# Placing the attention steps of a hybrid decoder block one by one

## The chip, the cores and the metric

The kernel runs on one core of a Trainium2 chip. That core has five instruction streams: PE (TensorE, matmuls and transpositions; its weight loads are listed apart as PEld), DVE (VectorE), ACT (ScalarE), POOL (GpSimd) and SP (SyncE, which issues DMAs). The metric is the device time of one execution in microseconds (us), as the median of several runs. One execution was also taken by the hardware profiler; its page and its trace are what the prediction reads.

## The reference, cut to what matters

One layer of a decoder on 1024 tokens of width 1024. The normalised input is multiplied by one wide matrix, which gives the queries and keys of a sparse attention (NSA), the inputs of a retention layer, and two merge gates. Both mixers' outputs are gated, summed and projected, then an MLP follows. The change is in the attention, which computes this for each block of 128 queries and each of two groups `g` of four heads:

```python
sc = jnp.einsum('qghd,cgd->gqhc', qi, k_cmp).astype(jnp.float32) * scale      # compressed keys
p_c = jax.nn.softmax(jnp.where(valid[None, :, None, :], sc, NEG), axis=-1)
o_c = jnp.einsum('gqhc,cgd->qghd', p_c.astype(dt), v_cmp)
...
ss = jnp.einsum('qghd,gqkd->gqhk', qi, k_sel).astype(jnp.float32) * scale     # selected blocks
p_s = jax.nn.softmax(jnp.where(smask, ss, NEG), axis=-1)
o_s = jnp.einsum('gqhk,gqkd->qghd', p_s.astype(dt), v_sel)
...
sw = jnp.einsum('qghd,kgd->gqhk', qi, k_win).astype(jnp.float32) * scale      # window of 512
p_w = jax.nn.softmax(jnp.where(wmask[None, :, None, :], sw, NEG), axis=-1)
o_w = jnp.einsum('gqhk,kgd->qghd', p_w.astype(dt), v_win)
o = gi[..., 0:1] * o_c + gi[..., 1:2] * o_s + gi[..., 2:3] * o_w
...
mix = sigmoid(gate_a) * (nsa_out @ w_proj_a) + sigmoid(gate_b) * (ret_out @ w_proj_b)
```

There are 16 blocks of 64 keys and 16 are selected, so the selected branch sees all keys up to the query's own.

## The kernel before, in words

Before the attention stage the kernel has normalised the input (`bh`, `bl`: high and low part, since one float32 product is made of three products of rounded parts), computed retention, queries, keys and values, and stored the queries to memory. After it come the last gate tiles, the two projections, the output projection, and the MLP.

The attention stage works on 16 *units*: `units` runs over the query blocks `qb` from 7 down to 0, and for each over the two groups `g`, so unit `n` has `qb = 7 - n // 2`. A unit has these steps.

*Query split* (`prep_q`, L1105 on ACT, L1106 on DVE): the query tile is split into `QQ` and `ql`. There are two buffers of each.

*Scores* (`scores`, generator). For each of four heads the selected branch (`base` 1, keys `KKs`) is made of one or two *score groups*, and then the window branch (`base` 2, keys `KKw`) likewise; a group is two matmuls into one PSUM tile `S` of at most 512 columns (`psS`, four buffers). The compressed keys of a block lie in `KKw` behind the window's, so the last window group covers them too; `put_cmp` copies them there (ACT) for each `qb`. For each part of a group DVE adds the mask and takes the minimum of the negated scores (`smallest`, L1161). For a head with two groups a small DVE instruction combines both minima (L1196). Then ACT takes the exponentials with that bias and sums them up (`exponential`, L1165), out of PSUM into the tiles `pSa`, `pSb`, `pW` and `pC`. After two heads of a branch come the *scalings* (`weigh_sel`, `weigh_win`): DVE makes a factor for each row from sums and gates (`factors`, L1211 to L1213), and POOL multiplies the probabilities by it (`weigh`, L1216). In the last two units (`qb` 0) one group holds all three branches of a head.

*Value blocks* (`pv`, generator). For each block of 128 keys, first of the selected branch and then of the window branch with the compressed block ahead of the last: four transpositions of the heads' probabilities into one PSUM tile `pt` (`psT`, two buffers, L1303), a split into `ph` (ACT, L1304) and `pl` (DVE, L1305), and `PV_LAG` = 2 blocks later the two matmuls with the values into `O`. At the end ACT and DVE copy `O` out into `AT` (L1316, L1320).

*Gate tiles* (`gate_pieces`): 32 tiles of 512 columns in eight pieces of three matmuls each, independent of the attention, fill PE between these steps. 244 of the 256 pieces lie in this stage. A tile accumulates in one PSUM buffer `gps`; from tile 17 on (`GALT`) every odd one takes a buffer of `S`. ACT drains it (L1067). At the sixth piece of a tile `gate_w` splits the next weight, once for two tiles: 1024 columns on ACT (L191) and on DVE (L194).

What sets the order. PE executes in the order in which the program was written. For the other engines a scheduler of the compiler puts instructions in order by when they can start, with program order deciding between those that are ready; instructions in `tc.keep_in_program_order` stay behind everything written for their engine before. These are the gate splits on ACT from the third weight on, the combined minima (L1196), and, where the selected branch has two groups, the first window minimum.

The program order itself comes from a list. `place(it, n, lo, hi)` sets `n` evenly spaced times between `lo` and `hi` (in units), at each of which the generator `it` is advanced by one step; the list `todo` is sorted by time and worked off. `S_AT` gives for each kind of unit, relative to the unit's number, begin and end of the selected groups and a time for their last scaling, and the same for the window's. The first scaling of a branch, the combined minimum and the exponentials are part of the generator's group steps. `GATES` says how many gate pieces lie in each unit, evenly spaced; `GATE0` how many come first; `Q_AT` and `C_AT` are the times of the query split and the key copy; `V_END` and `V_LAST` the end of the value blocks.

```python
for n, (qb, g) in enumerate(units):
    ...
    it = scores(n, qb, g, u)
    for k, (lo, hi, w) in zip(n_scores(qb), S_AT[min(n, 1 + (7 - qb))]):
        place(it, k - 1, n + lo, n + hi)
        place(it, 1, n + w, n + w)
    it = pv(qb, g, u)
    place(it, n_pv(qb) - 1, n, n + 1 + V_END)
    ...
for ev in sorted(todo, key=lambda v: v[:2]):
    ...
```

## Time and profile before

| | us |
|---|---|
| median of 3 runs (lowest, highest) | 1544.66 (1544.12, 1545.6) |
| time of the profiled execution | 1543.7 |
| its span, first to last instruction | 1541.5 |
| PE with a matmul, of the span | 1523.3 |
| DVE, ACT, POOL busy, of the span | 1038.4, 710.7, 515.1 |
| attention stage, on the span | 356.7 to 733.7 |
| PE, DVE, ACT, POOL busy in it | 368.7, 278.7, 258.2, 129.9 |

The time of an execution is a little longer than its span, by 2.2 us here. A matmul is listed with its latency, which overlaps the next one's; so PE's busy time says how much of the stretch had some matmul under way, and not how fast matmuls followed one another. Distances between starts say that. PEld is the weight load ahead of each matmul; a matmul that waits is often seen as a weight load that waits. In a list of waits the engine and line that waited stand left of the arrow, and what ended the wait right of it.

### The profile page before, as it was taken

How to read it: one execution, taken by the hardware profiler on the slowest of the kernel's cores; microseconds unless marked ns; L12 is line 12 of the kernel's file. 1: busy time of each engine (PE TensorE's matmuls, PEld its weight loads, DVE VectorE, ACT ScalarE, POOL GpSimd, SP SyncE). 2: the span in 40 equal slices, each digit the busy share in tenths (PEclk: the TensorE clock that was granted, in tenths of full speed). 3: DMA queues.
4: the chain of work that ended last, by engine and by line, in shares of the span. 5: the costliest groups of instructions: out<-in, count | busy, mean ns of one | idle time of the engine just before them, and what ended most of it. 6: DMA issues, size and time to landing. Idle time of an engine off the chain costs nothing.

```text
span 1541.5 us, 21817 instructions
## 1 busy us (share of the span) xinstructions
PE 1523.3 (99%) x7529; PEld 1269.1 (82%) x7529; DVE 1038.4 (67%) x2000; ACT 710.7 (46%) x1574; POOL 515.1 (33%) x567
## 2 busy tenths in 40 slices
PE   9999999999999999999999999999999999999998
PEld 6888888898888787788888888888888888888887
DVE  6865661666778777775754378876666768786573
ACT  6653462555677667775421263222222244443452
POOL 4110011002233333333000014767777518723640
PEclk9999999999999999999999999999999999999999
DMA  5202215752111111111644433444444797573472
GB/s 207 90 18 65 59 45 131 210 173 69 55 42 36 62 42 42 63 62 63 232 137 157 138 127 104 151 150 150 151 151 151 245 342 262 199 250 123 143 276 93
DMA packets 101904, 202.85 MB, mean 132 GB/s; under 512 B 10714, under 2 KB 27490, under 8 KB 101730
## 3 DMA queue, kind: packets, MB, share of 16 engines
q1 hardware_dynamic: 100946, 199.30, 39.0%
q0 software_dynamic: 704, 1.90, 0.3%
q8 instruction: 59, 0.97, 0.2%
q14 instruction: 51, 0.42, 0.1%
q10 hardware_dynamic: 144, 0.26, 0.0%
HBM read 147.75 MB, written 53.61 MB: 131 GB/s over the span
## 4 chain that ended last, share of the span: by engine, by line
PE 87%; DVE 5%; ACT 3%; issue 3%; POOL 2%; DMA 0%; SPq 0%; POOLq 0%; ACTq 0%; DVEq 0%
PE mm L164 24%; PE mmu L164 21%; PE mmd L164 20%; PE gps L164 9%; PE O L164 3%; PE S L164 3%; PE pt L1303 3%; DVE pl L1305 1%; ACT pW L1165 1%; PE pc L164 1%; PE pO L164 1%; DVE S L1161 1%; ACT ph L1304 1%; PE tp L397 0%; PE pS L164 0%
## 5 line engine op out<-in xcount | busy, mean ns | idle before, releaser
L1460 DVE TENSOR_TENSOR wl<-raw,wh 128x1024 fp32r<-128x1024 f32 x134 | 218.7, 1656 | 88.7 <-ACT wh L1459 88.5
L1459 ACT ACTIVATE wh<-raw 128x1024 fp32r<-128x1024 f32 x134 | 136.6, 1054 | 156.0 <-PE mmd L164 100.1
L164 PE MATMUL mmd<-wl,wh 128*128 128x512 f32 (+1 forms) x464 | 177.2, 382 | 0.0
L164 PE MATMUL mmd<-wh 128*128 128x512 f32 (+1 forms) x464 | 177.2, 382 | 0.0
L164 PE MATMUL mmd<-wh,wl 128*128 128x512 f32 (+1 forms) x464 | 177.1, 382 | 0.0
L200 POOL TENSOR_SCALAR msq<-ssq 128x1 f32<-128x1 f32 (+1 forms) x32 | 7.7, 241 | 387.9 <-ACT h L206 223.3
L1161 DVE CUSTOM_DVE_ANT_0 S<-S,edge_m 128x512 f32<-128x512 f32 (+9 forms) x200 | 101.7, 516 | 32.9 <-PE S L164 27.7
L164 PE MATMUL mm<-wh,bh 128*128 128x512 f32 (+1 forms) x320 | 122.4, 382 | 0.1
L164 PE MATMUL mm<-wl,bh 128*128 128x512 f32 (+1 forms) x320 | 118.9, 372 | 0.4 <-DVE wl L499 0.4
L164 PE MATMUL mm<-wh,bl 128*128 128x512 f32 (+1 forms) x320 | 118.0, 373 | 0.0
L1305 DVE TENSOR_TENSOR pl<-pt,ph 128x512 fp32r<-128x512 f32 (+1 forms) x148 | 97.4, 660 | 25.3 <-ACT ph L1304 23.1
L164 PE MATMUL gps<-bh,wh 128*128 128x512 f32 x256 | 107.9, 421 | 0.0
L1304 ACT ACTIVATE ph<-pt 128x512 fp32r<-128x512 f32 (+1 forms) x148 | 85.2, 578 | 39.5 <-PE pt L1303 38.3
L164 PEld LDWEIGHTS mmd<-wh 128*128 128x128 f32 x464 | 87.2, 188 | 17.1
L164 PEld LDWEIGHTS mmd<-wh,wl 128*128 128x128 f32 x464 | 87.2, 188 | 17.0
L164 PEld LDWEIGHTS mmd<-wl,wh 128*128 128x128 f32 x464 | 87.2, 188 | 16.7
L164 PE MATMUL mmu<-bh,wh 128*128 128x512 f32 (+1 forms) x264 | 101.0, 383 | 0.0
L164 PE MATMUL mmu<-bl,wh 128*128 128x512 f32 (+1 forms) x264 | 100.9, 383 | 0.0
L164 PE MATMUL mmu<-bh,wl 128*128 128x512 f32 (+1 forms) x264 | 100.6, 383 | 0.0
L164 PE MATMUL gps<-bh,wl 128*128 128x512 f32 x256 | 100.6, 393 | 0.0
L164 PE MATMUL gps<-bl,wh 128*128 128x512 f32 x256 | 100.5, 393 | 0.0
L1216 POOL TENSOR_SCALAR pSa<-pSa,cf 128x512 f32<-128x512 f32 (+2 forms) x52 | 32.9, 646 | 133.7 <-DVE cf L1213 99.0
(381 smaller groups left out, 3999.2 us busy)
## 6 DMA issues: line engine op xcount, KB each, us to landing
raw<-u_scr SPq DMA_DIRECT2D x56, 512.0 KB, 4.4
raw<-w_down SPq DMA_DIRECT2D x41, 512.0 KB, 5.2
raw<-w_up SPq DMA_DIRECT2D x32, 512.0 KB, 3.9
u_scr<-u SPq DMA_DIRECT2D x60, 256.0 KB, 4.1
u_scr<-s SPq DMA_DIRECT2D x45, 256.0 KB, 2.3
y<-w_down SPq DMA_DIRECT2D x16, 512.0 KB, 7.0
x<-x SPq DMA_DIRECT2D x8, 512.0 KB, 4.8
raw<-w_ga SPq DMA_DIRECT2D x8, 512.0 KB, 3.9
```

What stands on the lines that cost most here:

```text
L164: T.matmul(o, w, m, start=start, stop=stop)
L200: G.tensor_scalar(m[:, :w], ssq, 1.0 / n, EPS, op0=OP.mult, op1=OP.add)
L1161: return V.tensor_tensor_reduce(sc, sc, mk, -0.125, BIGPOS, OP.add, OP.min, mx[:, i, b:b + 1])
L1165: A.activation(o, sc, AF.Exp, bias=mx[:, i, m:m + 1], scale=-1.0, accum_out=sums[:, i, b:b + 1])
L1216: G.tensor_scalar(v, v, cf[:, i, b:b + 1], 1.0, op0=OP.mult, op1=OP.mult)
L1303: T.transpose(tp[:, k], ps[k if n == 2 else (0, 2, 1, 3)[k]], ident)
L1304: A.activation(ph[:, :n], tp[:, :n], AF.Copy)
L1305: V.tensor_sub(pl[:, :n], tp[:, :n], ph[:, :n])
L1459: A.activation(h[:, :n], r, AF.Copy)
L1460: V.tensor_sub(l[:, :n], r, h[:, :n])
```

## The change

The generator `scores` becomes a list of single steps with a time each. A score group (`group`: two matmuls, the minima, and for a head's last group the combined minimum), the exponentials of a head (`exponentials`) and each scaling of two heads (`weigh_sel`, `weigh_win`) are steps of their own. `S_AT` is now given for each `qb`, and `S_FIRST` for the first unit: begin and end of the selected groups, the times of their two scalings, the same for the window, and a delay for the exponentials of each branch after the head's last group. `Q_AT` and `C_AT` are lists by `qb`. `GATES` has other numbers with the same total (244 with `GATE0`, which is 1 instead of 2), and `GAP` compresses the eight pieces of a gate tile to seven eighths of their stretch, so that the gap to the next tile is wider. `V_END` is 0.0385 instead of 0.025. The pin on the first window minimum goes; that on the combined minima stays. The tiles for minima, sums and factors are allocated at first use. No instruction is added or removed.

```diff
-GATES = [14] + [16] * 8 + [12] * 6 + [14] * 2
-S_AT = [[(-0.95, -0.5, -0.4), (-0.4, 0.2, 0.3)],
-        [(-0.56, -0.18, -0.12), (-0.06, 0.3, 0.38)],
-        [(-0.57, -0.18, -0.12), (-0.07, 0.27, 0.34)],
-        [(-0.59, -0.18, -0.12), (-0.08, 0.24, 0.3)],
-        [(-0.62, -0.18, -0.12), (-0.09, 0.2, 0.25)],
-        [(-0.75, -0.4, -0.35), (-0.42, -0.05, 0.05)],
-        [(-0.75, -0.4, -0.35), (-0.42, -0.05, 0.05)],
-        [(-0.75, -0.45, -0.4), (-0.4, -0.14, -0.08)],
-        [(-0.75, -0.2, -0.12)]]
-C_AT = [0.45, 0.15]
-Q_AT = 0.1
-V_END = 0.025
-GATE0 = 2
-V_LAST = 0.025
+S_AT = {0: [[[-0.808, -0.207]], [-0.234, 0.047], [], [], [0.147, 0.033]],
+        1: [[[-0.588, -0.302]], [-0.444, -0.187], [[-0.35, -0.147]], [-0.15, -0.056], [0, 0.0]],
+        2: [[[-0.879, -0.346]], [-0.547, -0.373], [[-0.451, -0.081]], [-0.039, 0.05], [0, 0.06]],
+        3: [[[-0.75, -0.4]], [-0.34, -0.248], [[-0.42, -0.156]], [-0.146, -0.043], [0.036, 0]],
+        4: [[[-0.609, -0.191]], [-0.216, 0.007], [[-0.13, 0.139]], [0.094, 0.29], [0.0, 0.02]],
+        5: [[[-0.554, -0.166]], [-0.323, -0.004], [[-0.085, 0.156]], [0.203, 0.35], [0.022, 0.03]],
+        6: [[[-0.577, -0.184]], [-0.276, -0.067], [[-0.073, 0.235]], [0.146, 0.452], [0, 0.028]],
+        7: [[[-0.564, -0.17]], [-0.349, 0.012], [[-0.053, 0.311]], [0.18, 0.382], [0, 0.035]]}
+S_FIRST = [[[-0.95, -0.444]], [-0.419, -0.336], [[-0.428, 0.178]], [-0.015, 0.3], [0, 0.001]]
+C_AT = [0.099, 0.155, 0.287, 0.596, 0.336, 0.512, 0.637, 0.0]
+Q_AT = [0.023, 0.025, 0.123, 0.062, 0.226, -0.035, 0.285, 0.062]
+GATES = [15, 16, 16, 15, 14, 17, 16, 16, 14, 13, 12, 12, 12, 12, 14, 15, 14]
+GATE0 = 1
+GAP = 1
+V_END = 0.0384514
+V_LAST = 0.0233542
...
-                        r = smallest(i, sc, mk, b)
-                        if (i, b, gi) == (0, 2, 0) and split[1]:
-                            tc.keep_in_program_order(r)
...
+            def group(base, i, gi):
...
+                for b, w, mk in parts:
+                    sc = ps[:, off:off + w]
+                    off += w
+                    smallest(i, sc, mk, b)
+                    held.setdefault((base, i), []).append((b, sc, w, c0))
+                if last and split[base]:
+                    m = stat("mx", 5)[:, i, base:base + 1]
+                    tc.keep_in_program_order(V.tensor_tensor(m, m, stat("mx", 5)[:, i, base + 2:base + 3], op=OP.min))
+
+            def exponentials(base, i):
                 (new_sel if base == 1 else new_win)()
-                for b, sc, w, c0 in exps:
+                for b, sc, w, c0 in held.pop((base, i)):
...
+            def steps(fn, at, e_lag, e_fn, heads):
+                for k, (h, v) in enumerate(zip(heads, at)):
+                    yield v, lambda h=h: fn(*h)
+                    if k == len(heads) - 1 or heads[k + 1][-2] != h[-2]:
+                        yield v + e_lag, lambda h=h: e_fn(*h[:-1])
...
+            for base, at_, w_at, widths, fn, lag in ((1, sel_at, sel_w_at, sel_w, weigh_sel, lags[0]),
+                                                     (2, win_at, win_w_at, win_w, weigh_win, lags[1])):
+                heads = [(base, i, gi) for i in range(4) for gi in range(len(widths))]
+                yield from steps(group, spread(at_, len(heads)), lag, exponentials, heads)
+                for hp in range(2):
+                    yield w_at[hp], lambda hp=hp, fn=fn: fn(hp)
...
-                place(prep_q(qb, g), 1, n - 1 + Q_AT, n - 1 + Q_AT)
+                place(prep_q(qb, g), 1, n - 1 + Q_AT[qb], n - 1 + Q_AT[qb])
...
+            for v, fn in scores(n, qb, g, u):
+                todo.append((n + v, len(todo), fn))
...
-        for n, k in enumerate(GATES):
-            place(gate_it, k, n - 1, n)
+        ends = np.cumsum([GATE0] + GATES)
+        for k in range(GATE0, int(ends[-1])):
+            at_k = k - k % 8 + GAP / 2 + (k % 8 + 0.5) * (8 - GAP) / 8
+            todo.append((float(np.interp(at_k, ends, np.arange(len(ends)) - 1.0)), len(todo), gate_it))
```

The unit's list ends, for `qb` 0, with `all_three`, `three_exponentials` and `weigh_all` placed in the same way.

More of the change, by code (lines that the diff above doesn't have):

```diff
@@ L1136, in new, with stat @@
                 return [at.tile([P, 640 if t == "pW" else 512], F32, name=t, tag=t, bufs=PS_S) for t in tags[base]]
-            sums = few.tile([P, 4, 5], F32, name="sums")
-            mx = few.tile([P, 4, 5], F32, name="mx")
-            cf = few.tile([P, 4, 3], F32, name="cf")
+            few_t = {}
+            def stat(name, k):
+                if name not in few_t:
+                    few_t[name] = few.tile([P, 4, k], F32, name=name)
+                return few_t[name]
             gate = gts[:, qb, g * 12:g * 12 + 12].rearrange("p (h b) -> p h b", b=3)
@@ new lines, in scores @@
+            held = {}
+            def group(base, i, gi):
+                KK, start, width, widths = (KKs, 0, cS, sel_w) if base == 1 else (KKw, w0, cW, win_w)
+                c0, w = sum(widths[:gi]), widths[gi]
+                last = gi == len(widths) - 1
+                parts = [(base + 2 * gi, w, mask(c0, w, width, base == 2 and nw == 5))]
+                if base == 2 and last:
+                    parts.append((0, cC, cmp_m[:, 56 - 8 * qb:64]))
+                ps = psS.tile([P, 512], F32, name="S")
+                cols = slice(start + c0, start + c0 + sum(p[1] for p in parts))
+                o = ps[:, :cols.stop - cols.start]
+                mm(o, qs[qb, g][0][:, i], KK[:, g, cols], True, False)
+                mm(o, qs[qb, g][1][:, i], KK[:, g, cols], False, True)
+                off = 0
+                for b, w, mk in parts:
[6 more added lines that the diff above has]
+                    tc.keep_in_program_order(V.tensor_tensor(m, m, stat("mx", 5)[:, i, base + 2:base + 3], op=OP.min))
@@ L1206, in branch @@
                     exponential(i, sc, o, b)
-                yield
             def factors(h, b, bs):
+                sums, cf = stat("sums", 5), stat("cf", 3)
                 if split[b]:
@@ L1256, in scores, with all_three @@
-            for base, KK, start, width, fn in ((1, KKs, 0, cS, weigh_sel), (2, KKw, w0, cW, weigh_win)):
-                for i in range(4):
-                    it = branch(i, base, KK, start, width)
-                    next(it)
-                    if i == 2:
-                        fn(0)
-                    yield
-                    yield from it
-                fn(1)
-                yield
+            def all_three(i):
+                ps = psS.tile([P, 512], F32, name="S")
+                w = 2 * P + cC
+                mm(ps[:, :w], qs[qb, g][0][:, i], KKw[:, g, :w], True, False)
+                mm(ps[:, :w], qs[qb, g][1][:, i], KKw[:, g, :w], False, True)
+                tri = edge_m[:, 512:]
+                held[i] = [(1, ps[:, P + cC:w], tri), (2, ps[:, :P], tri), (0, ps[:, P:P + cC], cmp_m[:, 56:56 + cC])]
+                for b, sc, mk in held[i]:
+                    smallest(i, sc, mk, b)
@@ new lines, in three_exponentials, with weigh_all @@
+            def three_exponentials(i):
+                new_sel()
+                new_win()
+                outs = {1: sel[i][0][:, :P], 2: win[i], 0: pc(i)}
+                for b, sc, mk in held.pop(i):
+                    exponential(i, sc, outs[b], b)
+            def weigh_all(hp):
+                weigh_sel(hp)
+                weigh_win(hp)
+            def steps(fn, at, e_lag, e_fn, heads):
[3 more added lines that the diff above has]
+                        yield v + e_lag, lambda h=h: e_fn(*h[:-1])
@@ new lines, in spread @@
+            def spread(parts, k):
+                per = k // len(parts)
+                return [lo + (hi - lo) * (j + 0.5) / per for lo, hi in parts for j in range(per)]
+            sel_at, sel_w_at, win_at, win_w_at, lags = S_AT[qb] if n else S_FIRST
+            if qb == 0:
+                heads = [(i, 0) for i in range(4)]
+                yield from steps(lambda i, _: all_three(i), spread(sel_at, 4), lags[0], three_exponentials, heads)
+                for hp in range(2):
+                    yield sel_w_at[hp], lambda hp=hp: weigh_all(hp)
+                return
@@ L1371, in hybrid_block @@
                 put_cmp(ev[3])
+            elif callable(ev[2]):
+                ev[2]()
             else:
```

67 lines of the change are left out of this document (6 added, 61 removed).

## Prediction

> **What bounds the kernel now.** I read the page first, then a table by stage, then who waits for whom on PE inside the attention stage, then the chain of waits and the timeline at the longest waits. From the page:
>
> ```profile
> span 1541.5 us, 21817 instructions
> ...
> PE 1523.3 (99%) x7529; PEld 1269.1 (82%) x7529; DVE 1038.4 (67%) x2000; ACT 710.7 (46%) x1574; POOL 515.1 (33%) x567
> ```
>
> PE is the engine without room. The change touches only the order of work in the attention stage, which the table by stage sets between 356.7 and 733.7 us (start of the first and end of the last of its matmuls; the last gate tiles follow):
>
> ```profile
> core 0: us, PE busy (x) PEld busy (x) DVE busy (x) ACT busy (x) POOL busy (x), PEclk, DMA share, GB/s
> 356.70:733.70 377.00, 368.68 (x2007) 303.97 (x2007) 278.65 (x973) 258.15 (x760) 129.94 (x252) 1.00 0.17 54
> ```
>
> Here the granted clock is 1.00 of full, PE has 8.3 us without any matmul, and DVE (74%) and ACT (68%) are busy but not full. A matmul's bar is longer than the distance to the next one, so "busy" hides part of a wait. How long steps take back to back is read from starts and from unbroken pieces of the chain:
>
> ```profile
> 13.12 0.88 PE tp L521 x8
> 510.27 0.70 PE gps L164 x3
> ...
> 733.73 8.18 PE gps L164 x36
> ```
>
> That is 0.110 us for a 128-column transposition (0.44 for a block of four) and 0.23 us for a 512-column matmul, about 0.45 ns a column: 0.70 for a gate step of three, 0.46 for the pair of a value block, and two matmuls by the width for a score group. The PE order is the program's own, and it follows from the placement numbers in the code. I wrote out the steps of both kernels in that order (both have the same 2,004 matmuls up to the last value block) and added these durations: 362.7 us in each. So about 14 us of the 377 are waits and switches, and no order can gain more than that here.
>
> Where they are, by the waits of PE's weight loads, each row from its own stretch (434 to 470, 500 to 505, 530 to 535, 558 to 562, 585 to 589, 590 to 603, 603 to 630 and 630 to 742 us); the columns after the colon are total us, times, longest:
>
> ```profile
> PEld S L164 <- ACT pW L1165: 1.2, 2, 0.6
> PEld pt L1303 <- POOL pW L1216: 2.1, 2, 1.6
> PEld pt L1303 <- POOL pW L1216: 2.6, 2, 2.1
> PEld pt L1303 <- POOL pW L1216: 1.0, 2, 0.6
> PEld pt L1303 <- POOL pW L1216: 0.7, 2, 0.6
> PEld S L164 <- ACT pSb L1165: 1.0, 2, 0.9
> PEld S L164 <- ACT pSa L1165: 1.9, 2, 1.4
> PEld S L164 <- ACT pC L1165: 0.9, 1, 0.9
> ```
>
> Two kinds. In units 4 to 7 the first transposition of a window block waits until POOL has scaled the probabilities: 2.1 + 2.6 + 1.0 + 0.7 = **6.4 us**. And a score group waits for a PSUM buffer, that is, until the exponentials of an older head are done: 1.2 + 1.0 + 1.9 + 0.9 = **5.0 us**.
>
> The chain of waits shows what is late in the first two of the first kind:
>
> ```profile
> 498.05 1.01 ACT pW L1165 x4
> 499.72 1.07 ACT wh L191
> 500.81 1.23 DVE wl L194
> 502.78 1.58 POOL pW L1216 x2
> ...
> 529.10 1.06 ACT wh L191
> 530.19 1.23 DVE wl L194
> 532.93 1.58 POOL pW L1216 x2
> ```
>
> The split of the next gate weight sits on ACT (1.07) and DVE (1.23) just between the last window scores and the factors that POOL needs. The timeline of PE and DVE has unit 4's last window group there, and on DVE one more split, that of the query two units ahead:
>
> ```profile
> 497.05 0.32 PE L164 MATMUL S<-KKw,QQ 128*128 128x344 f32 x1
> ...
> 498.24 1.18 DVE L1106 TENSOR_TENSOR ql<-qt,QQ 128x512 fp32r<-128x512 f32 x1
> 502.42 0.16 DVE L1213 TENSOR_TENSOR cf<-cf,gts 128x4 f32<-128x4 f32 x1
> ```
>
> **The change, part by part.** No operation is added or removed; one pin on DVE goes (the first window minimum behind earlier work). So every term is a wait that goes or comes. "Slack" below is the sum of PE's step durations between two places of its order, without waits.
>
> *Scores earlier, scalings apart.* From the start of a unit's last window group to its first window transposition, the slack in units 2 to 7 was 6.6, 6.5, 5.1, 5.2, 5.2, 5.8 us, and becomes 7.8, 7.6, 7.4, 8.2, 6.8, 6.7. (Unit 5: the last group moves from 0.220 to 0.141 of a unit, the transposition from 0.468 to 0.474.) Only slacks of 5.1 to 5.8 stalled; 6.5 did not. The need can be added up at unit 4: its last group starts at 497.05, the factors end at 502.58 (5.5), the two scalings at 502.78 + 1.58 = 504.36, together 7.3. The gate split's step was 2.2 to 4.6 us ahead of the first window transposition in units 3 to 7 and is now between 2.6 ahead and 2.5 behind, after the factors; without it the need is 7.3 - 1.2 = 6.1. All four units now have more slack than that: **-6.4, of which I take -6.2**, since units 6 and 7 have only 0.6 us to spare. The other bound is that only the gate split's part goes: 1.2 in each of units 4 and 5, 0.6 in 6 and 7 together, or -3.0.
>
> *Score groups closer together.* There are four buffers for score groups, and a group frees its buffer when its head's exponentials are read. What one head costs ACT, and a transposed block ACT and DVE (groups by line; after the bar busy us and mean ns):
>
> ```profile
> L1165 ACT ACTIVATE pW<-S,mx 128x352 f32<-128x352 f32 (+7 forms) x88 | 44.9, 516 | 15.6 <-DVE mx L1196 8.6 <-DVE mx L1161 5.0 <-POOL pSb L1216 1.2
> L1165 ACT ACTIVATION_READ_ACCUMULATOR pW<-S,mx 128x1 f32 x88 | 17.7, 201 | 0.0
> L1165 ACT ACTIVATE pC<-S,mx 128x64 f32<-128x64 f32 (+7 forms) x64 | 18.8, 293 | 0.0
> L1304 ACT ACTIVATE ph<-pt 128x512 fp32r<-128x512 f32 (+1 forms) x148 | 85.2, 578 | 39.5 <-PE pt L1303 38.3 <-ACT QQ L1105 0.3
> L1305 DVE TENSOR_TENSOR pl<-pt,ph 128x512 fp32r<-128x512 f32 (+1 forms) x148 | 97.4, 660 | 25.3 <-ACT ph L1304 23.1
> ```
>
> A split window head is two exponentials of 0.5, a small one of 0.3, and 0.2 to read each of three sums, near 1.9 us of ACT, beside 0.58 for each transposed block. I measured the slack of each group against the head that held its buffer. Before, the stalls of 0.9 and 1.4 lie at slacks of 1.6 (unit 8) and 1.4 (unit 9), that of 0.9 at 2.3 (unit 13); 2.6 mostly went unpunished; 3.4 was punished only in units 2 and 3 (0.6 each), where a unit's closing copies on ACT and DVE fall among the window heads. After: unit 8 has 2.1, 2.3, 2.1, 1.6 and a gate tile that takes the same buffers at 1.4, its eight groups start within 5.1 us where it was 7.7; unit 12 has 1.6, 1.9, 1.9; unit 9 improves to 2.6 at worst, unit 13 to 2.6; units 2 to 5 have 2.7 to 3.4 around the closing copies. I price unit 8 at 1.8, unit 12 at 1.2 (one wait pushes the rest back, so they don't add), units 2 to 5 at 0.55 each and the others at 0.3: 5.5 against 5.0, **+0.5**. Lower bound: all waits of this kind go but one like unit 13's, 0.9 - 5.0 = -4.1. Upper: every group of units 8 and 12 pays its whole shortfall to 3.4, which is 1.3 + 1.1 + 2.0 + 1.3 + 1.8 and 0.6 + 1.8 + 1.5 + 1.5 + 0.8, 13.7 instead of 3.0: +11.2.
>
> *Value blocks.* They run a little later, and with other steps between them. Two PSUM tiles hold transposed blocks; one is free 0.58 + 0.66 us after a transposition and its hand-overs, some 1.5. The smallest slack was 2.1; now the third block of units 0, 3 and 1 has 1.5, 1.8 and 1.9. **+0.8**, between 0 and 2 (0.6 each and a little elsewhere).
>
> *Later scalings of the selected branch.* The second pair's step moves from 3.7 to 4.2 us ahead of the first transposition in units 4 to 7 to 1.5, in unit 1 from 3.9 to 0.8.
>
> ```profile
> L1216 POOL TENSOR_SCALAR pSa<-pSa,cf 128x512 f32<-128x512 f32 (+2 forms) x52 | 32.9, 646 | 133.7 <-DVE cf L1213 99.0
> ```
>
> Were the factors issued no earlier than their step, the data would be there three small DVE instructions like the 0.16 above and two scalings of 0.65 later, 1.8 us: 1.0 late in unit 1 and 0.3 in the four others; for the window branch of units 2 and 3, with 1.5 and 1.9 us left and 2.1 needed, 0.8 in all. But DVE, ACT and POOL are put in order by readiness: the trace has work far ahead of its step, like the query split above, which belongs a unit later. On the other side, the window minima now stand ahead of the factors, and the pinned minimum of a window head no longer stands behind factors that wait for ACT. **+0.5**, between 0 and 3.0.
>
> *Gate tiles with a gap, the first tile's start, copies of compressed keys, query splits.* A tile's first matmul waits for the drain of the one before:
>
> ```profile
> PEld gps L164 <- ACT gst L1067: 0.8, 3, 0.4
> ```
>
> So at best -0.8; the gap costs no PE work, as other steps fill it. Query splits and key copies are hoisted by readiness in any case; DMAs that they issue (the load two queries ahead) land long before. **0**, between -0.8 and +0.5.
>
> Sum: -6.2 + 0.5 + 0.8 + 0.5 = **-4.4**. The profiled execution took 1543.7 us, so 1539.3; the median of the runs, 1544.66, lies 1.0 above it, so 1540.3.
>
> One rule of the Trainium skill speaks against moving scalings. On the row 498.24 above, the query split took 1.18 us where its median is 0.70, while POOL was scaling; a gate split did the same:
>
> ```profile
> L1106 DVE TENSOR_TENSOR ql<-qt,QQ x16: 678/702/1189, 354.9 to 694.9; 128x512 fp32r<-128x512 f32 x16
> L194 DVE TENSOR_TENSOR wl<-raw,wh x32: 1215/1226/1756, 68.5 to 872.3; 128x1024 fp32r<-128x1024 f32 x32
> ```
>
> The excess is 0.5 us each. The Trainium skill, SBUF — State Buffer, section "Who interferes with whom", says that a DVE instruction with two SBUF inputs and a GpSimd instruction that reads SBUF exclude one another; the trace agrees with that by those 0.5 us.
>
> **The rivals.** *Scalings still late* (20%): the query split stays where it was, because readiness places it, and only the gate split's share goes: -3.0 + 0.5 + 0.8 + 0.5 = -1.2, 1543.5. For it: 1.18 of the 5.5 us at unit 4. Against: the added slack is larger than that split.
>
> *Buffers in units 8 and 12* (15%, slower): 13.7 instead of 3.0 there, -4.4 + 10.7 = +6.3, 1551.0. For it: a window head every 1.5 us of PE against 1.9 us of ACT. Against: earlier shortfalls cost about a third of their size. It makes the change slower than no difference from about 7.5 us above my 3.0.
>
> *DVE and POOL in each other's way* (5%): gate splits now come just after the factors in units 3 to 7, where POOL scales; 0.54 (1.756 less 1.215) for each of five, all on PE's path: +2.7, 1543.0. It is the rule named above made to cost PE time; no wait of PE now shows it.
>
> *More than forecast* (8%): the buffer waits go as well, -4.4 - 4.6 = -9.0, 1535.7.
>
> **How the numbers follow.** The forecast has 52%, with 1537 to 1541.5 as its own range. This kernel's measurement can't tell less than 0.2%, 3.1 us, from no change: faster is below 1541.6, slower above 1547.8. Forecast and "more" are faster, 60%; the two middle rivals the same, 25%; buffers slower, 15%. The range leaves out the end of "more" and most of the slower case: 1536.5 to 1547.0.
>
> **What would show it.** Right: in the changed profile no wait of PE for POOL's window scaling above 0.3 us in units 4 to 7; score groups waiting for ACT in units 8 and 12, together near 3 us; the stage from the first gate matmul to the end of the last value block near 372.6 instead of 377.0 us; the time before and behind it unchanged. Wrong: waits for the window scaling still above 3 us (then the query split or the place of the factors holds them), score groups waiting over 10 us, or a stage shorter by 4 us and an end that isn't.

## The result, and the profile after

The changed kernel takes 1535.82 us (median of 4 runs, 1535.68 to 1536.35), against 1544.6 us for the kernel before (1544.12 to 1545.6). The ratio is 0.9943, with a 95% interval of 0.9926 to 0.996. It is faster by 8.8 us, twice the 4.4 us forecast, and just below the range that was given. The profiled execution of the changed kernel took 1536.35 us, 0.5 above its median; that of the kernel before took 1543.7, 0.9 below its own. Between the two traces, which the accounts below read, the difference is therefore 7.35 us.

The page of the changed kernel has the same amount of work and a shorter span:

```profile
span 1534.3 us, 21815 instructions
...
PE 1521.7 (99%) x7529; PEld 1270.9 (83%) x7529; DVE 1036.3 (68%) x2000; ACT 707.0 (46%) x1574; POOL 510.9 (33%) x567
```

The table by stage, from the first gate matmul to the end of the last value block (from, to and length of the stretch, then the busy times of PE, PEld, DVE, ACT and POOL, the granted clock, the DMA share and GB/s):

```profile
356.90:726.00 369.10, 365.76 (x2007) 305.21 (x2006) 277.41 (x973) 254.97 (x760) 127.40 (x252) 1.00 0.18 55
```

The stage is 7.9 us shorter (377.0 before), with the same matmuls and the same granted clock. The time behind it is unchanged: 1541.5 - 733.7 = 807.8 us before, 1534.3 - 726.0 = 808.3 now. The gain lies where the change is, and nearly all of it is made of waits. The waits of PE's weight loads between 350 and 742 us, by what ended them (total us, times, longest), in the changed kernel:

```profile
PEld S L165 <- ACT pSb L1169: 1.7, 2, 1.5
PEld pt L1315 <- ACT gst L1068: 1.1, 1, 1.1
PEld pt L1315 <- POOL pW L1217: 1.0, 2, 0.6
PEld pt L1315 <- PE S L165: 0.8, 1, 0.8
```

and in the kernel before, in the same stretch:

```profile
PEld pt L1303 <- POOL pW L1216: 6.5, 8, 2.1
PEld S L164 <- ACT pW L1165: 2.2, 6, 0.6
PEld S L164 <- ACT pSa L1165: 1.9, 2, 1.4
```

The waits for the window scaling went from 6.5 to 1.0 us. One place is left, in unit 7; one score group waits for its buffer for long, in unit 8; and two transpositions wait, in units 0 and 3. The timeline of the changed kernel shows these four (start, duration, engine, operation; in brackets how long the engine had been idle and what ended it):

```profile
374.24 0.60 ACT L1068 ACTIVATE gst<-gps 128x512 f32<-128x512 f32 x1
...
374.89 0.65 PE L1315 MATMUL pt<-ident,pSa 128*128 128x128 f32 x4 [0.85 <-ACT gst L1068]
...
462.43 0.69 DVE L1317 TENSOR_TENSOR pl<-pt,ph 128x512 fp32r<-128x512 f32 x1
...
463.27 0.63 PE L1315 MATMUL pt<-ident,pSa 128*128 128x128 f32 x4 [0.53 <-DVE pl L1317]
...
576.45 0.16 DVE L1212 TENSOR_TENSOR sums<-sums 128x2 f32<-128x2 f32 x1
576.53 0.69 DVE L1165 CUSTOM_DVE_ANT_0 S<-S,edge_m 128x512 f32<-128x512 f32 x1
...
577.14 0.17 DVE L1213 RECIPROCAL cf<-sums 128x4 f32<-128x4 f32 x1
577.35 0.69 DVE L1317 TENSOR_TENSOR pl<-pt,ph 128x512 fp32r<-128x512 f32 x1
577.95 0.15 DVE L1214 TENSOR_TENSOR cf<-cf,gts 128x4 f32<-128x4 f32 x1
...
578.30 1.57 POOL L1217 TENSOR_SCALAR pW<-pW,cf 128x640 f32<-128x640 f32 x2 [5.18 <-PE S L165]
...
588.85 0.39 PE L165 MATMUL S<-KKw,QQ 128*128 128x272 f32 x1 [1.22 <-ACT pSb L1169]
```

In unit 0 the gap leaves no gate piece between the first two blocks. The second gate tile lies in one of the two PSUM buffers of the transpositions; its drain on ACT ends at 374.84, and the second block's transposition, which takes that buffer, starts at 374.89. In unit 7 the three small factor instructions, 0.16 us each, take 1.65 us from first to last, because a minimum of unit 8 and a value split lie between them. (In unit 3 the transposition waits for the split of the block two before it, at 462.43.)

For the account below I took, in every kernel, the distance from the start of each step of PE to the start of the next, less the step's own duration, and added up what exceeds 0.25 us. "Window" is a transposition waiting for a scaling on POOL, nearly always the window's, "buffer" a score group or a gate tile waiting for a PSUM buffer, "blocks" a transposition or a matmul of a value block waiting for ACT or DVE. The lists of PEld waits count the same waits from the loads and without the limit, so their sums differ by some tenths, in one kernel by 1.1 us.

| kernel | time, us | window | buffer | blocks | sum |
|---|---|---|---|---|---|
| before | 1544.6 | 6.1 | 4.5 | 1.0 | 11.6 |
| after | 1535.8 | 0.9 | 1.9 | 2.2 | 5.0 |
| after, gates' places of before | 1538.7 | 2.2 | 4.1 | 1.3 | 7.6 |
| after, score groups' places of before | 1537.7 | 1.7 | 2.5 | 2.2 | 6.4 |
| after, both of these | 1539.5 | 5.3 | 1.9 | 1.5 | 8.7 |
| after, value blocks' ends of before | 1542.3 | 2.8 | 4.6 | 3.1 | 10.5 |
| before, new ends alone | 1541.4 | 4.5 | 4.8 | 0.8 | 10.1 |
| before, new ends and new gates | 1539.6 | 1.6 | 3.3 | 3.7 | 8.6 |
| after, two places mended | 1533.3 | 0.9 | 0.7 | 1.5 | 3.0 |

The sums fall by 6.6 us from before to after, of the 7.9; the rest is in waits below 0.25 us.

### The profile page after: what moved, and what is told of

It is laid out like the page before. It is cut to its first block, busy times and chain, and to the rows that moved or that the text cites. A ratio compares the mean times of both kernels' runs of the same rounds, so it can differ in the third digit from the quotient of the medians.

```text
span 1534.3 us, 21815 instructions
## 1 busy us (share of the span) xinstructions
PE 1521.7 (99%) x7529; PEld 1270.9 (83%) x7529; DVE 1036.3 (68%) x2000; ACT 707.0 (46%) x1574; POOL 510.9 (33%) x567
## 4 chain that ended last, share of the span: by engine, by line
PE 92%; DVE 3%; issue 3%; POOL 1%; ACT 1%; DMA 0%; POOLq 0%; SPq 0%; DVEq 0%; ACTq 0%
PE mm L165 24%; PE mmu L165 20%; PE mmd L165 20%; PE gps L165 11%; PE O L165 4%; PE S L165 4%; PE pt L1315 4%; PE pc L165 1%; PE pO L165 1%; PE pD L165 0%; PE tp L398 0%; PE pS L165 0%; PE tp L522 0%; DMA x1t<-x_scr 0%; POOL rstd L202 0%
## 5 line engine op out<-in xcount | busy, mean ns | idle before, releaser
L1165 DVE CUSTOM_DVE_ANT_0 S<-S,edge_m 128x512 f32<-128x512 f32 (+8 forms) x200 | 101.9, 516 | 32.2 <-PE S L165 28.6
```

The source lines that it names most:

```text
L1165: return V.tensor_tensor_reduce(sc, sc, mk, -0.125, BIGPOS, OP.add, OP.min, stat("mx", 5)[:, i, b:b + 1])
```

## The experiments

Each kernel below is the changed kernel with the edit shown, unless it says otherwise. It is compared with 1535.8 us.

**Gates as before.** Numbers and even spacing of the gate pieces go back.

```diff
-GATES = [15, 16, 16, 15, 14, 17, 16, 16, 14, 13, 12, 12, 12, 12, 14, 15, 14]
-GATE0 = 1
+GATES = [14] + [16] * 8 + [12] * 6 + [14] * 2
+GATE0 = 2
...
-            at_k = k - k % 8 + GAP / 2 + (k % 8 + 0.5) * (8 - GAP) / 8
...
+        for n, k in enumerate(GATES):
+            place(gate_it, k, n - 1, n)
```

> The changed kernel with the gate pieces placed as before (old GATES and GATE0, no gap). The split of a gate weight falls again 2 to 4.6 us ahead of the first window transposition in units 3 to 7. Theory A (the score groups' earlier place gives the slack, the split's place is a help): slack there is 8.1, 8.2, 6.8, 7.4 us in units 4 to 7 against a need of 7.3 with the split, so at most 1 us of window-scaling waits; the waits for a transposition tile in units 0 and 3 go (-1.9); buffers in units 8, 9 and 13 get worse by 1 to 2; in all 1535 to 1537.5. Theory B (the split's place is what took the window-scaling waits away): they come back with about 5 us, 1540 to 1542.

Measured: 1538.72 us (ratio to before 0.9963, 0.995 to 0.9976), 2.9 us more, between the two theories. The gates were priced at nothing; undone, their places cost about a third of the gain. Most of it is buffers, 4.1 us instead of 1.9: score groups of units 8 and 9 wait 2.4 us. The waits in units 0 and 3 are gone. Window waits come back in units 4 to 7 (0.36, 0.89, 0.33, 0.28 us), and not for want of slack, which is 8.1, 8.2, 6.8 and 7.4 us there against 7.4, 8.2, 6.8 and 6.7 in the changed kernel. In units 4 and 5 POOL itself takes longer. The timeline of this kernel in units 4 and 5, and below it unit 5 in the changed one:

```profile
499.49 2.54 POOL L1217 TENSOR_SCALAR pW<-pW,cf 128x640 f32<-128x640 f32 x2 [0.20 <-PE pt L1315]
499.85 1.51 DVE L195 TENSOR_TENSOR wl<-raw,wh 128x1024 fp32r<-128x1024 f32 x1
...
524.84 1.22 DVE L195 TENSOR_TENSOR wl<-raw,wh 128x1024 fp32r<-128x1024 f32 x1 [0.18 <-ACT wh L192]
524.85 2.66 POOL L1217 TENSOR_SCALAR pW<-pW,cf 128x640 f32<-128x640 f32 x2 [7.93 <-ACT wh L192]
```

```profile
524.38 1.57 POOL L1217 TENSOR_SCALAR pW<-pW,cf 128x640 f32<-128x640 f32 x2 [9.12 <-PE pt L1315]
```

Two scalings take 1.57 us alone, and 2.54 and 2.66 where a gate split on DVE has begun just before one of them. (In unit 6 the scaling began first, and the split took 1.78 us instead of 1.22.) The 1.0 us more is longer than either wait: in unit 4 the transposition waits for these two scalings, in unit 5 for the next two, which start later by it. So in these units the old place of the gate split brings the waits back, as the second theory had it, though with 1.3 us and not 5.

**Scalings as before.** The two scalings of each branch go back to the distance from the score groups that they had.

```diff
...
-                for hp in range(2):
-                    yield w_at[hp], lambda hp=hp, fn=fn: fn(hp)
+                ts = spread(at_, len(heads))
+                per = len(widths)
+                first = max(ts[2 * per], ts[2 * per - 1] + lag)
+                last = max(ts[-1] + W_OLD[n and 8 - qb][base - 1], ts[-1] + lag)
+                for hp, v in enumerate((first, last)):
+                    yield v + 1e-6, lambda hp=hp, fn=fn: fn(hp)
```

> The changed kernel with both scalings of each branch put where they were before, as seen from the score groups (the first with the third head's first group, the second 0.05 to 0.15 of a unit after the last group). Theory A (factors written ahead of the pinned minima hold DVE up until ACT has its sums, and with it the buffers): waits of score groups come back in units 2 to 5 and 9, 2 to 4 us, DVE's idle time before the sums grows, 1538 to 1540. Theory B (DVE and POOL are put in order by readiness, so the place of a scaling in the list does nothing): 1535.8 within 0.7 and the same waits.

Measured: 1535.39 us (0.9941, 0.9927 to 0.9956), with the same waits, as the second theory had it. POOL's instructions come in the same order in both traces, and DVE's in nearly the same. That scalings are set apart has no share in the gain.

**Score groups as before.** The begin and end of the selected and window groups go back, the scalings' times stay.

```diff
...
-        7: [[[-0.564, -0.17]], [-0.349, 0.012], [[-0.053, 0.311]], [0.18, 0.382], [0, 0.035]]}
...
+        7: [[[-0.56, -0.18]], [-0.349, 0.012], [[-0.06, 0.3]], [0.18, 0.382], [0, 0.035]]}
...
```

> The changed kernel with begin and end of the score groups as before, everything else new. Window slack in units 2 to 7 is 6.6, 7.2, 6.5, 6.6, 5.9, 5.8 us against a need of 6.1 without the gate split. Theory A (scalings and split apart are most of the gain, the groups' place a part): waits for the window scaling of 0.3 to 1 us in units 6 and 7 only, buffer waits in unit 8 down from 1.9 to about 1; 1535.5 to 1537.5. Theory B (the groups' earlier place is the gain): the window-scaling waits are back at 4 us or more, 1539.5 to 1542.

Measured: 1537.71 us (0.9957, 0.994 to 0.9973), 1.9 us more, just above the first theory. The window waits are 1.7 us instead of 0.9, and gate tiles 17 and 19, which take a buffer of `S`, wait 1.6 us.

**Gates and groups as before.** Both edits above.

> The changed kernel with both the gate pieces and the score groups placed as before; what is left of the change is the steps apart, the exponentials' delay, the pin and the later value blocks. One of them undone cost 3.3 and one 2.3 us. Theory A (each covers for the other: a window scaling is late only where the gate split is in its way and the group is late): slack 5.8, 5.9, 5.2, 5.8 in units 4 to 7 against 7.3 needed, 5 us or more of window-scaling waits, the buffer waits of before, 1542.5 to 1545. Theory B (the parts add): 1535.6 + 3.3 + 2.3 = 1541.2, and what is left, some 3.5 us, belongs to the steps apart, the pin or the ends.

Measured: 1539.5 us (0.9968, 0.9956 to 0.9981), 3.7 us more, which is neither number and less than 2.9 + 1.9. The waits for POOL are 5.3 us, but 1.0 of them by the list of PEld waits is for scalings of the selected branch, where the kernel before had none, and the score buffers stay at 1.9 us. So 5.1 us of the gain are still there without either.

**The rest as before.** Key copies, query splits and the ends of the value blocks go back.

```diff
-C_AT = [0.099, 0.155, 0.287, 0.596, 0.336, 0.512, 0.637, 0.0]
-Q_AT = [0.023, 0.025, 0.123, 0.062, 0.226, -0.035, 0.285, 0.062]
+C_AT = [0.15] * 2 + [0.45] * 6
+Q_AT = [0.1] * 8
...
-V_END = 0.0384514
-V_LAST = 0.0233542
+V_END = 0.025
+V_LAST = 0.025
```

> The changed kernel with the old times of query splits and key copies and the old ends of the value blocks. Window slack falls in units 3, 4, 6 and 7 to 6.7, 6.9, 6.0 and 6.3 us (need 6.1 without the gate split). Theory A (the later end of the value blocks is what gives these units their spare time): 0.5 to 1 us more window-scaling waits, 1536 to 1537.5. Theory B (query split and copies are placed by readiness, the value blocks' end is small): 1535.6 within 0.7.

Measured: 1543.39 us (0.9993, 0.9984 to 1.0003), beyond both theories. With these three settings undone, nearly the whole gain is gone, though all score, scaling and gate places are the new ones. The next three runs take them one by one.

**Key copies, query splits, ends.** One of the three edits each.

> The changed kernel with the old times of the key copies alone (C_AT); queries and value blocks new. The three old together cost 7.8 us. Theory A (the pinned gate split on ACT hangs behind the one instruction written before it; with the old times that is the key copy in units 3 and 5, which runs early, and the split with it): in those two units the split on DVE comes about 2.7 us after the last window group instead of 7 to 8, with waits of 2 to 2.5 us in unit 3 and 1.5 in unit 5 and nothing elsewhere; 1538.5 to 1540. Theory B (a copy is placed by readiness, so its place in the list does nothing): 1535.6 within 0.7.

> The changed kernel with the old time of the query splits alone (Q_AT). Theory A (the query split is placed by readiness, and no pinned instruction of units 3 to 7 hangs behind it): 1535.6 within 0.7. Theory B (with program order deciding among ready work, an earlier query split goes ahead of factors and copies): 2 to 4 us more, 1537.5 to 1539.5, in units 2 to 7.

> The changed kernel with the old ends of the value blocks alone (V_END, V_LAST). Window slack falls to 6.7, 6.9, 8.0, 6.0, 6.3 in units 3 to 7, and the last window group of unit 3 has 2.2 us for its buffer where it had 2.7. Theory A (these are the rest of the 7.8): waits of 0.5 to 1 each more in units 2, 3, 6 and 7, 2.5 to 4 us, 1538 to 1539.5. Theory B (0.7 us of slack is not short yet): 1535.6 within 0.7.

Key copies: 1536.67 us (0.9948, 0.9933 to 0.9963); its runs (1536.06 to 1537.35) overlap those of the changed kernel, so 0.9 us is at most a hint, and the 1538.5 of the first theory isn't reached. The mechanism that was expected is there, without most of the waits. The timeline with the old key copies and, below it, with the new ones (unit 5, whose last window group starts 520.1 and 519.5 us after the span's start):

```profile
521.33 0.30 ACT L1341 ACTIVATE KKw<-KKw 128x80 fp32r<-128x80 f32 x1
521.49 1.09 ACT L192 ACTIVATE wh<-raw 128x1024 fp32r<-128x1024 f32 x1
522.44 0.57 ACT L1169 ACTIVATE pW<-S,mx 128x344 f32<-128x344 f32 x1
...
522.88 1.21 DVE L195 TENSOR_TENSOR wl<-raw,wh 128x1024 fp32r<-128x1024 f32 x1
...
529.36 0.33 PE L1315 MATMUL pt<-ident,pW 128*128 128x128 f32 x1 [0.22 <-POOL pW L1217]
```

```profile
520.81 0.30 ACT L1341 ACTIVATE KKw<-KKw 128x80 fp32r<-128x80 f32 x1
...
526.45 1.05 ACT L192 ACTIVATE wh<-raw 128x1024 fp32r<-128x1024 f32 x1
...
527.66 1.46 DVE L195 TENSOR_TENSOR wl<-raw,wh 128x1024 fp32r<-128x1024 f32 x1
```

With the old places the key copy is the last ACT instruction written before the pinned gate split; it runs early, the split follows it, and it stands in front of the window factors. The price is one wait of 0.44 us, as unit 5 now has 8.2 us of slack. In unit 3 the split comes 2.5 us earlier too, and no wait of the 2 to 2.5 us expected there appears.

Query splits: 1535.58 us (0.9941, 0.9925 to 0.9958), nothing.

Ends: **1542.34 us** (0.9984, 0.9974 to 0.9993), 6.5 us more, beyond both theories. One number moves the last value blocks of a unit by 0.0135 of a unit, which is 0.36 us of 26.9, and their first ones by less (`V_LAST` moves only the very last step of all units); and it takes three quarters of the gain. The waits of PE's weight loads in that kernel:

```profile
PEld pt L1315 <- POOL pW L1217: 3.9, 6, 1.4
PEld S L165 <- ACT pW L1169: 2.7, 3, 1.6
PEld S L165 <- ACT pSb L1169: 1.9, 2, 1.5
PEld pt L1315 <- PE S L165: 1.8, 4, 0.8
```

Two things make up most of it. In units 6 and 7 the slack of the window scaling falls from 6.8 and 6.7 to 6.0 and 6.3 us, and waits of 0.95 and 1.85 us stand there instead of 0 and 0.88. And in units 2 and 3 a value block changes places with a score group. The timeline of unit 3 with the old ends:

```profile
462.65 0.60 PE L1315 MATMUL pt<-ident,pSa 128*128 128x128 f32 x4
...
463.25 0.33 PE L165 MATMUL S<-KKw,ql 128*128 128x348 f32 x1
...
463.57 0.69 DVE L1317 TENSOR_TENSOR pl<-pt,ph 128x512 fp32r<-128x512 f32 x1 [0.60 <-ACT ph L1316]
...
464.19 0.85 DVE L1332 TENSOR_TENSOR AT<-O,gst 64x256 f32<-64x256 f32 x2
...
465.07 0.69 DVE L1317 TENSOR_TENSOR pl<-pt,ph 128x512 fp32r<-128x512 f32 x1
...
465.68 0.46 DVE L1165 CUSTOM_DVE_ANT_0 S<-S,edge_m 128x292 f32<-128x292 f32 x1
...
466.95 0.55 ACT L1169 ACTIVATE pW<-S,mx 128x348 f32<-128x348 f32 x1 [1.22 <-DVE mx L1196]
...
467.64 0.43 PE L165 MATMUL S<-KKw,QQ 128*128 128x348 f32 x1 [1.14 <-ACT pW L1169]
```

and the same head with the new ends, in the changed kernel:

```profile
461.67 0.33 PE L165 MATMUL S<-KKw,ql 128*128 128x348 f32 x1
...
461.83 0.60 PE L1315 MATMUL pt<-ident,pSa 128*128 128x128 f32 x4
...
462.03 0.47 DVE L1165 CUSTOM_DVE_ANT_0 S<-S,edge_m 128x292 f32<-128x292 f32 x1 [0.20 <-PE S L165]
```

With the new ends the head's second score group stands ahead of a transposed block, and its minimum runs as soon as the matmuls end (462.00). With the old ends the block is ahead, and when the group's matmuls end (463.58) DVE already has the block's split, the closing copies of the unit before and a second split to do. The minimum starts 2.1 us late, the exponentials follow, and a later group waits 1.3 us for a buffer. The Trainium skill, PSUM — Partial Sum Buffer, section "Engine vs sequencer instructions", says that the queues of ScalarE, VectorE and GpSimdE are strictly first in, first out. The trace agrees here: the minimum could run from 463.58, DVE takes the three instructions ahead of it at 463.57, 464.19 and 465.07, and it starts at 465.68.

**The pin.** The first window minimum is pinned again.

```diff
-                    smallest(i, sc, mk, b)
+                    r = smallest(i, sc, mk, b)
+                    if (i, b, gi) == (0, 2, 0) and split[1]:
+                        tc.keep_in_program_order(r)
```

> The changed kernel with the pin on the first window minimum put back in the units with two groups in the selected branch. Theory A (the pin made DVE wait in order, and cost buffer waits in units 2 to 5): those waits return, 1.5 to 4 us, 1537 to 1540. Theory B (the minimum would stand behind that work anyway): 1535.6 within 0.7.

Measured: 1535.94 us (0.9947, 0.9932 to 0.9962): nothing.

**Is it the ends alone, and where?** The first kernel is the one before with the new ends, the second the one before with new ends and new gates, and the third the changed one with the old end in units 4 to 15 only.

```diff
-V_END = 0.0384514
+V_END = [0.0384514] * 4 + [0.025] * 12
...
-            place(it, n_pv(qb) - 1, n, n + 1 + V_END)
+            place(it, n_pv(qb) - 1, n, n + 1 + V_END[n])
```

> The kernel before with one thing changed: the end of the value blocks at the new place (V_END 0.0385, V_LAST 0.0234). Theory A (the value blocks' place is worth what it takes from each wait by itself): it gains most of what undoing it lost in the changed kernel (6.6 us), 1538 to 1541. Theory B (the place is only worth something beside the new score and gate places, because the value blocks' own times there just miss the score groups): alone it gives the 0.5 us of slack that it moves, 1543 to 1546, with the window-scaling waits of units 4 to 7 still near 5 us.

> The kernel before with the new end of the value blocks and the new gate places (GATES, GATE0, GAP), its scores and scalings as they were. In the changed kernel undoing the ends cost 6.6 us and undoing the gates 3.1. Theory A (these two carry the gain, whatever the scores do): 1535.5 to 1538.5. Theory B (the gain needs the score places too, since the window scalings stay at 5.1 to 5.8 us of slack in units 4 to 7): 1541 to 1545, with window-scaling waits of 4 us or more.

> The changed kernel with V_END 0.025 in units 4 to 15 only; units 0 to 3 keep 0.0385. With it old everywhere the time was 1542.3, with waits of 3.6 us in units 2 and 3 and 6.9 in units 4 to 9. Theory A (the effect is local, each unit pays for its own value blocks): 1542.3 less 3.6 less the small rest, 1538.5 to 1539.5, with the waits of units 6 to 8 unchanged near 4.3 us. Theory B (the waits of units 2 and 3 are made by the order as a whole): they come back elsewhere, 1541 to 1543.

Ends alone: 1541.42 us (0.9981, 0.9972 to 0.9991), 3.4 us below the 1544.83 us of before in that comparison; neither theory, about half of the 6.5. The slack of the window scaling grows by 0.7 us in units 4 and 5 (5.1 to 5.8, 5.2 to 5.9), and the waits shrink by the same: 1.97 to 1.26 and 2.61 to 1.90. The score buffers don't gain (4.5 and 4.8 us), since the blocks that changed places with score groups above do so only beside the new score places; in unit 3 the order of PE is the same here as in the kernel before.

Ends and gates: 1539.56 us (0.9969, 0.9958 to 0.998), again between. The slacks become 6.5, 6.6, 5.9 and 5.8 us in units 4 to 7 and the window waits 1.6 us in all, with the score groups where they were; the rival's 4 us or more is wrong. The waits of PE's weight loads in the two kernels show it:

```profile
PEld pt L1303 <- POOL pW L1216: 4.9, 7, 1.5
```

```profile
PEld pt L1304 <- POOL pW L1217: 2.0, 5, 0.6
```

Old end in the later units: 1539.26 us (0.9967, 0.9954 to 0.998), within the numbers of the local theory. In units 1 to 3, where the old end had cost 3.2 us of waits, only the 0.77 us of unit 3's transposition are left, which the changed kernel has too; the waits of units 6, 7 and 8 stay (0.94, 1.84, 1.46). Each unit pays for its own order.

So, added in this order to the kernel before (1544.8 us there), the ends bring 3.4 us, the gates 1.9, and the score groups with the rest 3.7. Taken from the changed kernel one at a time they are worth 6.5, 2.9 and 1.9. The shares depend on the order in which they are taken; that the second three add up to 11.3 us, more than the whole gain, shows that they help each other.

**What is left, and can it be taken?** Four places mended at once: no gap in the first three gate tiles (unit 0), the window groups of `qb` 3 (units 8 and 9) spread wider, those of `qb` 4 (units 6 and 7) earlier, and one gate piece a unit earlier, for unit 3.

```diff
-        3: [[[-0.75, -0.4]], [-0.34, -0.248], [[-0.42, -0.156]], [-0.146, -0.043], [0.036, 0]],
-        4: [[[-0.609, -0.191]], [-0.216, 0.007], [[-0.13, 0.139]], [0.094, 0.29], [0.0, 0.02]],
+        3: [[[-0.75, -0.4]], [-0.34, -0.248], [[-0.42, -0.04]], [-0.1, 0.04], [0.036, 0]],
+        4: [[[-0.609, -0.191]], [-0.216, 0.007], [[-0.17, 0.1]], [0.07, 0.25], [0.0, 0.02]],
...
-GATES = [15, 16, 16, 15, 14, 17, 16, 16, 14, 13, 12, 12, 12, 12, 14, 15, 14]
+GATES = [15, 16, 16, 16, 13, 17, 16, 16, 14, 13, 12, 12, 12, 12, 14, 15, 14]
...
-GAP = 1
+GAPS = [0] * 3 + [1] * 28 + [0]
...
```

> The changed kernel with four places moved where its profile still shows PE waiting: no gap ahead of tile 2 (unit 0 waits 1.1 us for a transposition tile that a gate tile holds), tile 8's first piece ahead of unit 3's third block (0.8), units 6 and 7's window groups 0.04 of a unit earlier (0.9), units 8 and 9's window groups spread over 0.38 instead of 0.264 of a unit (1.9). If these waits are lost time: 3 to 4.5 us less, 1531.5 to 1533. If they are filled by what runs behind them: 1535.8 within 0.7.

Measured: 1537.17 us (0.9954, 0.9939 to 0.9969), 1.4 us worse. The waits in units 0 and 7 went, unit 8's became one of 0.66 us for a gate tile, unit 3's one of 0.50; and others came: 0.97 us ahead of unit 1's last value block, 0.90 for gate tile 19, and 1.23 and 1.55 us in units 6 and 7. The timeline of unit 6 shows the split of the first blocks behind a closing copy and a gate drain on ACT:

```profile
546.33 0.59 ACT L1328 ACTIVATE gst<-O 64x512 f32<-64x512 f32 x1
...
546.95 0.60 ACT L1068 ACTIVATE gst<-gps 128x512 f32<-128x512 f32 x1
547.44 1.08 ACT L1316 ACTIVATE ph<-pt 128x512 fp32r<-128x512 f32 x2
...
548.05 0.47 PE L165 MATMUL O<-ph,VV 128*128 128x512 f32 x1 [0.98 <-ACT ph L1316]
```

Then only the first two (the window groups in unit 8 alone; the edit follows), and these two with another gap in gate tile 8 (-0.2 instead of 1), near unit 3's transposition, as a third.

```diff
+S_8 = [[[-0.75, -0.4]], [-0.34, -0.248], [[-0.42, -0.04]], [-0.1, 0.04], [0.036, 0]]
...
-GAP = 1
+GAPS = [0] * 3 + [1] * 28 + [0]
...
-             sel_at, sel_w_at, win_at, win_w_at, lags = S_AT[qb] if n else S_FIRST
+             sel_at, sel_w_at, win_at, win_w_at, lags = (S_8 if n == 8 else S_AT[qb]) if n else S_FIRST
...
```

> The changed kernel with two of the four fixes: no gap ahead of tile 2 (unit 0's wait of 1.1) and unit 8's window groups alone spread over 0.38 of a unit (1.9 to about 0.7). Units 1 to 7 and 9 keep their order. If each wait is lost time: 2 us less, 1533.2 to 1534.3. If what follows takes them up again: 1535.6 within 0.7.

> The kernel with two fixes (1533.3) and a third: tile 8's first piece ahead of unit 3's third value block, by the gap of that tile alone. If the 0.8 us wait there is lost time and nothing new comes up: 1532.3 to 1532.9. If it only moves: 1533.3 within 0.5.

Two places: **1533.3 us** (1533.11 to 1533.56; 0.9929, 0.9914 to 0.9944), faster than both kernels and 2.5 us below the changed one. Its page and its stage:

```profile
span 1531.2 us, 21815 instructions
```

```profile
356.60:723.60 367.00, 365.29 (x2008) 304.84 (x2008) 276.46 (x973) 255.10 (x761) 126.87 (x252) 1.00 0.17 55
```

Three places: 1533.8 us (1533.59 to 1533.94; 0.9929, 0.9914 to 0.9944), no better. Unit 3's 0.79 us went, and a new window wait of 0.38 us and small ones came.

**Later still.** The kernel with two places mended, with `V_END` 0.052.

> The kernel with the gap left out of the first three gate tiles and unit 8's window groups spread (1533.3 us), with V_END still later, 0.052 instead of 0.0385. By the slacks alone (theory A) the last close pair of transpositions, unit 3's 0.79 us, goes, and nothing else gets below its need: 1532.0 to 1533.5. Theory B (0.0385 fits the other numbers, and any other value makes new collisions of score groups and blocks): 1535 to 1540.

Measured: 1534.63 us (0.9937, 0.9921 to 0.9954), 1.3 us more, between the two. Later is not simply better. A transposition of unit 1 now waits 0.5 us for its scaling, and unit 3's wait, which by the distance between its transpositions should have gone, is 0.77 us. The split of the block whose buffer it takes stands on ACT behind a window head's exponentials, which that distance does not see.

## Why the prediction was right or wrong

**What bounds the kernel** was right: PE has no room, the work is the same, the stage alone changed, and the two kinds of wait named are the ones that fell.

**"Score groups closer together"** (+0.5) is the term that failed: it came to -2.6. Of the 3.5 us between the forecast of -4.4 and the -7.9 of the stage, that is 3.1. Unit 8 was right (1.9 us against 1.8). Unit 12, for which I took 1.2 us, and units 2 to 5, for which I took 2.2, have no buffer wait above 0.25 us. I priced each slack by the waits seen at about that slack before, 0.55 us for 2.7 in units 2 to 5. What decides in unit 3 is the order of one transposition and one score group, which makes 0 of it with the new ends (slack 2.7) and 1.3 with the old (2.2). The lower bound, -4.1, did hold it.

The reading behind this term was too long as well. The 1.9 us of ACT for a split window head adds up bars that overlap. The timeline of the changed kernel has the first of a head's six instructions and, below it, what follows them on ACT:

```profile
523.35 0.55 ACT L1169 ACTIVATE pW<-S,mx 128x344 f32<-128x344 f32 x1
...
524.64 0.60 ACT L1316 ACTIVATE ph<-pt 128x512 fp32r<-128x512 f32 x1
```

That is 1.3 us, less than the 1.5 us of PE that I set against it. A window head of `qb` 1, the kind of unit 12, has no second group and takes 0.8 (680.70 to 681.52). So ACT keeps up with the window heads where nothing else stands in its queue, which fits the absence of waits in unit 12; no run varies it.

**"Scores earlier, scalings apart"** (-6.2) came to -5.2 by the account above. The waits of units 4 to 6 are gone, unit 7 keeps 0.88, where I had said that none above 0.3 would be left. The need at unit 4 was well read: slack and wait add up to 7.1 us there both before and with the new ends alone. The need without the gate split was taken as 6.1 us for all units, and that was too low: unit 7 has 6.7 and waits 0.88, and with the old ends units 6 and 7 have 6.0 and 6.3 and wait 0.95 and 1.85, needs of 7.0 to 8.2. DVE puts the next unit's minima and value splits between the factors, as the rows at 576.45 to 577.95 show. The step's name was wrong as to the cause: the scalings' places do nothing, and the slacks that I added up were made by score groups, gate pieces and value blocks together. With the score groups' old places alone the window waits are 1.7 us, with the old ends 2.8.

**"Value blocks"** (+0.8) was right in the size: the transpositions of units 0 and 3 wait 1.10 and 0.77 us, unit 1's not at all, and all waits of this kind grow by 1.2. In unit 0 it's a gate tile that holds the buffer, not an older block. What the term left out is the other side: moving the blocks later also moves what stands between other steps, and in what order score groups and blocks reach DVE. Alone that is worth 3.4 us, and in the changed kernel 6.5; a part of it stood, without this name, in the slacks of the window scaling, and the part that takes buffer waits away stood nowhere.

**"Later scalings of the selected branch"** (+0.5): nothing came; with the old places of the scalings the time is the same.

**"Gate tiles with a gap, the first tile's start, copies of compressed keys, query splits"** (0): query splits right, key copies right within what can be told, gates wrong. Undoing the gates' places costs 2.9 us. I took "other steps fill the gap" for "costs and brings nothing", but with the pieces' old places 2.2 us of buffer waits come back, and a gate split runs beside POOL's scalings in units 4 and 5, where PE then waits 1.3 us. In the first three tiles the gap costs, as the 1.10 us in unit 0 show.

**The rivals.** "Scalings still late" didn't happen, nor did "buffers in units 8 and 12". "DVE and POOL in each other's way" cost no PE time in the changed kernel: of the gate splits in units 3 to 5 two took longer than their 1.22 us,

```profile
L195 DVE TENSOR_TENSOR wl<-raw,wh x3: 1225/1301/1455, 473.9 to 527.7; 128x1024 fp32r<-128x1024 f32 x3
```

but none of their users waited. Its mechanism is what the gates' old places bring back, with POOL as the one that is held up. "More than forecast" (1535.7) gives the time to 0.1 us, which is luck. Its mechanism, buffer waits that go as well, came to 3.1 of the 4.6 us that it took, and waits below 0.25 us fell by another 1.3; but the window scaling gave 1.0 less than it assumes, and 1.4 of the 8.8 us lies in where the medians stand about the profiled executions.

**What stays open.** Why ends alone bring 3.4 us between medians when the waits over 0.25 us shrink by only 1.5 is not settled: the profiled executions are 2.5 us apart (1541.21 against 1543.7), their stages 2.1, and the rest is within the spread of single runs (1541.21 to 1542.67, and 1543.39 to 1546.4 for before). The window waits of units 6 and 7 with the gates' old places (0.33 and 0.28 us) are not explained either.

## What to carry to other kernels

When one engine is full and executes in program order, as PE does here, every piece of its work is also the distance between its neighbours: a step that is moved should be priced by what lies between others before and after, and by what it puts beside them on other engines, not only by what it waits for itself. Here 0.36 us of shift in one number was worth 6.5 us, and the order of one transposition against one score group on DVE decided 1.3 of them. Mend such waits one at a time and time each: two mends brought 2.5 us, these two with a third brought no more, and four at once lost 1.4.

## What was not expected

- A slack is not a price. In unit 3 a score group with 2.7 us to its buffer waits 0 and one with 2.2 waits 1.3, since a late minimum is 2.1 us late at once, by whole instructions of DVE ahead of it, and not by the half microsecond that the slack lost.
- An instruction kept in program order was tied only to the one written just before it on its engine, and not to everything written before, as the kernel's description says. With the old key copies the gate split started on ACT 5.0 us earlier (521.49 against 526.45), following a 0.30 us copy that readiness had moved, and ahead of exponentials of its unit (522.44) that stand before it in the list.
- Two window scalings of POOL took 1.57 us alone, and 2.54 and 2.66 where a gate split had begun just before one of them on DVE. In the changed kernel none of the window scalings of units 4 to 7 is lengthened by a gate split.
- The shares of parts of one reordering are not additive: gates and groups undone cost 2.9, 1.9 and together 3.7 us, the ends 6.5 where the whole change brings 8.8.
